# Norm weight in the evacuation, and sums spread between splits: two seams of a transformer layer kernel

## The chip, the cores and the metric

The kernel runs on one core of one Trainium2 chip. A core has a matrix engine (TensorE, PE below), a vector engine (VectorE, DVE), a scalar engine (ScalarE, ACT), GpSimd (POOL) and a queue engine (SyncE, SP), which work side by side, each in the order of its own instructions, and wait for each other by semaphores. SP and POOL issue the transfers (DMA) between HBM and the on-chip memory SBUF. PE writes its results into PSUM, from which ACT or DVE must fetch them ("evacuate") before the buffer is used again. The metric is the device time of one execution in microseconds (us).

## The reference

One layer of a streaming encoder runs on 1024 prompt tokens and 32 sample tokens, which share the weights. All numbers are fp32. Cut to what matters here:

```python
def rms_norm(x, g):
    xf = x.astype(jnp.float32)
    y = xf * lax.rsqrt(jnp.mean(xf * xf, axis=-1, keepdims=True) + EPS) * g.astype(jnp.float32)
    return y.astype(x.dtype)

def conv_ffn(h, conv_s0, w_up, conv_w, conv_b, w_down):
    a, g = jnp.split(h @ w_up, [D_FF], axis=-1)
    gx = jnp.concatenate([conv_s0.astype(g.dtype), g], axis=1)
    gc = conv_b + sum(conv_w[i] * gx[:, i:i + T] for i in range(CONV_W))
    y = (jax.nn.gelu(gc) * a) @ w_down
    return y, gx[:, T:]

def layer_forward(...):
    ...
    mix = (jax.nn.sigmoid(ga) * (oa @ w_br_a) + jax.nn.sigmoid(gb) * (ob @ w_br_b)) @ w_out
    x = x + rms_norm(mix, g_post_mix)
    f, conv_new = conv_ffn(rms_norm(x, g_pre_ffn), conv_s0, w_up, conv_w, conv_b, w_down)
    x = x + rms_norm(f, g_post_ffn)
    gate = jax.nn.sigmoid(rms_norm(x, g_pre_ple) @ w_ple_gate)
    x = x + rms_norm(gate * (pe @ w_ple), g_post_ple)
```

D_MODEL is 1024 and D_FF 2816. Ahead of this stand a gated linear attention and a banded softmax attention, which the change does not touch.

## The kernel before

Activations lie transposed: features on the 128 partitions, the 1056 tokens along the free axis. Where tokens are cut, there are three chunks of 352 (NC = 3, CW = 352) or two halves of 528, each taken as 2 x 264. PE multiplies fp32 as high and low parts: a value is split by ACT into a rounded high part (h, hi, mh, whi) and by DVE into the rest (l, lo, ml, wlo), and a product is three matmuls (high by high, high by low, low by high). A product of eight feature tiles is thus 24 matmuls.

**The out stage** (L1714 to L1739) computes z = mix @ w_out chunk by chunk, eight products a chunk (n = 0 to 7), with all of a chunk's z in one tile. Each product goes into one of four rotating PSUM buffers ("mm"). ACT copies it to z[:, n]; after each second product ACT squares the pair (L1607) and DVE adds the square to an accumulator. At the end of the chunk the generator norm_steps is made for it. It runs in 16 steps, called out of the next chunk's product loop by OUT_STEPS (so many steps after product n) and, for the last chunk, out of the plain up products by UP_STEPS. The steps are: the loads of the residual and the total of the accumulator (fold, L1621, and its split, L1632 and L1633); the inverse root (two matmuls with a matrix of ones that sum over partitions, L1638 and L1639, then log, exp and a Newton step, with a table load of ACT ahead, L239); four steps that multiply a pair of z's tiles by weight and root (times, L1656), add the residual (L1670) and square the result; the last square; its total; an empty step; the second inverse; four steps that multiply by the next norm's weight, spill z to d_hn, and split it into the rows of the up products (L1691 for the high part, L1685 for the low); and the last low part. Engines' orders are written out by hand here (manual_schedule for PE, DVE and ACT); SP's and POOL's come from a scheduler.

**The plain up products** follow (up_plain): the first three pairs of up tiles (f = 0 to 2; j = 0, 1 for the two halves of w_up), chunk by chunk, from the rows hh and hl. Out of their loop run the last chunk's norm and then plain_rest, which loads d_hn again (tiles hn, pool sp) and forms the quarter sums t1, t2 (and later t3, t4) for what comes next. The pool zp, with z, is released just before sp is made.

**The up stage** (up_strassen, f = 4 to FT - 1) multiplies quarters with seven products in place of eight. A product here is 24 matmuls of 264 columns into a PSUM pair (X, Y, Z, V, U). The activated rows go to HBM (d_b) for the down stage.

**The last up pair** (f = FT - 1) has a written order of its own: after X, Y, Z come V (rows t2), U (rows t1), and V again with t3 added. Eight DVE additions from PSUM finish it, three between the products (L1946, L1947, L1949) and five in a function ends() (L1953, L1954 and last_quarter, L1921 to L1923).

**The down stage** begins by loading rows (row_load, into sraw and uraw) and weights (w_load, raw and wraw) and splitting them (row_split: ACT L2050, DVE L2051, tiles d0 to d8; w_split: ACT L2099, DVE L2100). Rows (0, 0) and (0, 1) go into a buffer of the pool sw, the others into uraw, a tile of pool rp that exists only when the pools sp and mp have been released. Then 28 products u of 66 matmuls each run, 22 row tiles by 3 (L2356 to L2358).

Of the kernel before, what the change touches and what calls it, by code (L numbers as in the profile page):

```python
# [17 lines left out]
P = 128  # L18
# [84 lines left out]
RES_BUFS = 4  # L103
OUT_STEPS = (1, 1, 2, 2, 2, 1, 1, 5)
UP_STEPS = (1, 1, 2, 2, 2, 1, 1, 2, 3)

# [7 lines left out]
def emit(tc, a):  # L114
# [1511 lines left out]
    def norm_steps(tmp, c, z, acc, g, resid, keep, g_next, dst, spill=None):  # L1626
# [9 lines left out]
        def inverse(out, h, l):  # L1636
            ps = ps_one()[:, :CW]
            pe.matmul(ps, ones["D"], h, start=True, stop=False)  # L1638
            pe.matmul(ps, ones["D"], l, start=False, stop=True)  # L1639
            log_exp()  # L1640
            newton(out, ps, tmp)
# [11 lines left out]

        def times(i, g, r):
            for j in range(2):
                ve.scalar_tensor_tensor(zs[i][:, j], zs[i][:, j], col(g + 2 * i + j), r, op0=ALU.mult, op1=ALU.mult)  # L1656
# [63 lines left out]
    for c in range(NC):  # L1720
        s = chunk(c)
        z = tl(zp, [P, KT, CW], tag="z", bufs=2)
        acc = tl(zp, [P, 2, CW], tag="accz", bufs=1)
        for n in range(KT):
            hi, lo = wout[n]
            ps = ps_mm()
            product(ps[:, :CW], hi, lo, [(k, k) for k in range(KT)], lambda k: mh[:, k, s], lambda k: ml[:, k, s])
            if c == 0:
                out_weights(n + 2)
            else:  # L1730
                norm_part(OUT_STEPS[n])
            if c == NC - 1 and n in (4, 5):
                up_weights(0, n - 4)
            ac.activation(z[:, n], ps[:, :CW], AF.Copy)
            if n % 2:
                squares(zp, acc, n // 2, z[:, n - 1 : n + 1])
        norm = norm_steps(zp, c, z, acc, G_POST_MIX, a["x"], d_x1, G_PRE_FFN,
                          lambda i, s=s: [t[:, 2 * i : 2 * i + 2, s] for t in (hh, hl)], d_hn)
    wo.release()  # L1739

# [64 lines left out]
    def up_plain():  # L1805
        bufs = {}
        steps = [(f, j, c) for cs in ((0, 1), (2,)) for f in range(3) for j in range(2) for c in cs]

# [25 lines left out]
    def quarter_rows(k):  # L1834
        b = [tl(sp, [P, T], tag="hn", bufs=2) for i in range(2)]
        dma.dma_start(b[0], d_hn[k])
        dma.dma_start(b[1][:, two], d_hn[k + HK, :, two])
        return b[0][:, one], b[0][:, two], b[1][:, two]
# [6 lines left out]
    def quarter_sums():  # L1845
        for n in ("t1", "t2"):
            XS[n] = [tl(sp, [P, HK, HT], F32R, tag=n + x) for x in "hl"]
        for k in range(HK):
            b11, b12, b22 = quarter_rows(k)
            t1, t2 = [tl(sp, [P, HT], tag="xs", bufs=2) for i in range(2)]  # L1850
            ve.tensor_tensor(t1, b12, b11, op=ALU.subtract)
            ve.tensor_tensor(t2, b22, t1, op=ALU.subtract)
            dma.dma_start(d_t2[k], t2)
            quarter_split("t1", k, t1)
            quarter_split("t2", k, t2)
            yield

    def quarter_third():
        XS["t3"] = [tl(sw, [P, HK, HT], F32R, tag="t3" + x) for x in "hl"]
        for k in range(HK):  # L1860
            t = tl(sp, [P, T], tag="hn", bufs=2)
            dma.dma_start(t[:, one], d_hn[k, :, two])
# [6 lines left out]
    def quarter_last():  # L1869
# [4 lines left out]
        for k in range(HK):  # L1874
            t = tl(sp, [P, T], tag="hn", bufs=2)
            dma.dma_start(t[:, one], d_t2[k])
# [7 lines left out]
    def up_strassen(f):  # L1884
# [46 lines left out]
        if f == FT - 1:  # L1931
# [11 lines left out]
            V, U = ps_pair(), ps_pair()  # L1943
            V_, U_ = V[:, :, :HC], U[:, :, :HC]
            mul(V, weight(s2, WL_ENG[1]), "t2", True, True)
            ve.tensor_tensor(q, p1, V_, op=ALU.add)  # L1946
            ve.tensor_tensor(c12, c12, q, op=ALU.add)  # L1947
            mul(U, weight(s1, WL_ENG[2]), "t1", True, True)
            ve.tensor_tensor(c12, c12, U_, op=ALU.add)  # L1949
            mul(V, weight(s3, WL_ENG[4]), "t3", False, True)  # L1950

            def ends():
                ve.tensor_tensor(q, p1, V_, op=ALU.add)  # L1953
                ve.tensor_tensor(c21, c21, q, op=ALU.add)  # L1954
                last_quarter(q, U)

            return gx, av, ends
        Y = ps_pair()
# [18 lines left out]

    sp = None


    def plain_rest(bufs):
        nonlocal sp
        zp.release()
        sp = pool("sp", side="right")
        yield from quarter_sums()
        activate(0, *bufs[0, 0])
# [20 lines left out]
    order.__exit__(None, None, None)  # L2007
    quarter_last()
    for f in (2, 3):
        activate(f, *open_[f, 0])  # L2010
# [27 lines left out]
    def row_load(p, i):  # L2038
        if p < len(RSRC):
            n = 2 if i < 5 else 1  # L2040

            raws[p, i] = (sw_raw() if (p, i) < (0, 2) else tl(rp, [P, 2 * HT], tag="uraw", bufs=3)).rearrange("p (k t) -> p k t", k=2)[:, :n]
            dma.dma_start(raws[p, i], d_b[RSRC[p], 2 * i : 2 * i + n].rearrange("k p t -> p k t"))
# [251 lines left out]
    for i in range(1, 5):  # L2295
        row_load(0, i)
    for q in range(3):
        row_split(0, q)
        w_split(0, q)
    row_load(0, 5)  # L2300
    row_split(0, 3)
    row_load(1, 0)
    last_up[2]()
    row_split(0, 4)
    row_load(1, 1)
    sw.release()
    last_rows_up = activate_steps(FT - 1, *last_up[:2])
# [374 lines left out]
```

## Time and profile before

| | |
|---|---|
| runs | 1953.86, 1954.07, 1955.78 us, median 1954.07 |
| profiled execution | 1952.56 us, of which 1950.6 are the span of the trace |
| granted TensorE clock | 0.996 |
| PE busy | 1898.7 us, 97% of the span, 13960 matmuls |
| DVE busy | 1284.8 us, 66% |
| ACT busy | 931.5 us, 48% |
| POOL busy | 208.0 us, 11% |
| DMA | 300.91 MB, mean 154 GB/s |

In the span the out stage lies at about 1045 to 1140 us, the last up pair ends at about 1606 us, and the first down product follows at once. A row of an engine in order of time gives start, duration, engine, line, operation, output and inputs with shapes, and in brackets the idle time ahead of it with what ended it. Durations overlap on PE, since matmuls are pipelined; distances are read from starts. A row of PE's waits gives the line that waited, what it waited for, the total in us, how many times, and the longest.

### The profile page before, as it was taken

What the parts mean: (1) busy time and instruction counts of PE and PEld (TensorE: products, weight loads), DVE (VectorE), ACT (ScalarE), POOL (GpSimd) and SP (SyncE); (2) the same over time, 40 slices, a digit from 0 to 9 for tenths busy, and PEclk for the clock granted to TensorE, in tenths of its full rate; (3) what the DMA queues carried; (4) which work ended last, traced back from release to release, by engine and by line L of the source; (5) the groups of instructions that cost most, each with busy time, mean ns of one, the idle gap of its engine ahead of it and who ended that gap; (6) DMA issues with size and microseconds to landing.
All of it is one profiled execution on the core that took longest, in us unless ns stands there. A gap on an engine that the chain in (4) does not pass through costs nothing.

```text
span 1950.6 us, 34919 instructions
## 1 busy us (share of the span) xinstructions
PE 1898.7 (97%) x13960; PEld 1861.5 (95%) x13960; DVE 1284.8 (66%) x2367; ACT 931.5 (48%) x1820; POOL 208.0 (11%) x352
## 2 busy tenths in 40 slices
PE   8999999999999999999999999999999999999996
PEld 8999999989999999999999999999999999999996
DVE  6855444555656776777544686877777766558776
ACT  7444345556665455453333455433334345555555
POOL 0000000000001101001220121111111211000112
PEclk9999999999999999999999999999999999999998
DMA  7233335232315546567844246544354559897756
GB/s 279 85 100 111 99 104 156 82 89 81 91 47 154 145 120 160 161 182 216 303 133 127 90 162 205 185 138 138 113 125 111 125 146 304 266 297 240 239 158 106
DMA packets 111119, 300.91 MB, mean 154 GB/s; under 512 B 12452, under 2 KB 34796, under 8 KB 110316
## 3 DMA queue, kind: packets, MB, share of 16 engines
q1 hardware_dynamic: 81500, 205.95, 33.5%
q0 software_dynamic: 28016, 88.05, 16.7%
q10 hardware_dynamic: 1440, 4.69, 0.6%
q8 instruction: 109, 1.79, 0.4%
q14 instruction: 54, 0.44, 0.1%
HBM read 201.20 MB, written 114.09 MB: 162 GB/s over the span
## 4 chain that ended last, share of the span: by engine, by line
PE 76%; DVE 12%; ACT 7%; issue 2%; DMA 2%; ACTq 0%; SPq 0%; DVEq 0%
PE two L1911 6%; PE two L1913 6%; PE two L1912 6%; PE mm L230 5%; PE mm L232 5%; PE mm L231 5%; PE mm L804 4%; PE mm L805 4%; PE mm L806 4%; PE two L2358 4%; PE two L2357 4%; PE two L618 4%; PE two L619 3%; PE two L2356 3%; PE two L620 3%
## 5 line engine op out<-in xcount | busy, mean ns | idle before, releaser
L804 PE MATMUL mm<-xh,whi 128*128 128x352 f32 x696 | 236.6, 340 | 0.0
L806 PE MATMUL mm<-xh,wlo 128*128 128x352 f32 x696 | 225.3, 324 | 0.0
L805 PE MATMUL mm<-xl,whi 128*128 128x352 f32 x696 | 224.6, 323 | 0.0
L2357 PE MATMUL two<-d,whi 128*128 128x264 f32 x616 | 174.8, 284 | 2.7 <-DVE d L2051 2.7
L2358 PE MATMUL two<-d,wlo 128*128 128x264 f32 x616 | 175.5, 285 | 1.2 <-DVE wlo L2100 1.2
L2356 PE MATMUL two<-d,whi 128*128 128x264 f32 x616 | 174.7, 284 | 0.1
L1913 PE MATMUL two<-mh,wlo 128*128 128x264 f32 x576 | 163.0, 284 | 0.0
L1912 PE MATMUL two<-ml,whi 128*128 128x264 f32 x576 | 162.9, 284 | 0.0
L1911 PE MATMUL two<-mh,whi 128*128 128x264 f32 x576 | 161.2, 284 | 0.0
L804 PEld LDWEIGHTS mm<-xh,whi 128*128 128x128 f32 x696 | 131.3, 189 | 1.7
L805 PEld LDWEIGHTS mm<-xl,whi 128*128 128x128 f32 x696 | 131.2, 189 | 0.4
L806 PEld LDWEIGHTS mm<-xh,wlo 128*128 128x128 f32 x696 | 130.5, 188 | 0.0
L2357 PEld LDWEIGHTS two<-d,whi 128*128 128x128 f32 x616 | 115.8, 188 | 3.3 <-DVE d L2051 3.3
L2358 PEld LDWEIGHTS two<-d,wlo 128*128 128x128 f32 x616 | 115.6, 188 | 1.7 <-DVE wlo L2100 1.7
L2356 PEld LDWEIGHTS two<-d,whi 128*128 128x128 f32 x616 | 116.4, 189 | 0.3 <-ACT d L2050 0.3
L1913 PEld LDWEIGHTS two<-mh,wlo 128*128 128x128 f32 x576 | 108.4, 188 | 0.0
L1912 PEld LDWEIGHTS two<-ml,whi 128*128 128x128 f32 x576 | 108.4, 188 | 0.0
L1911 PEld LDWEIGHTS two<-mh,whi 128*128 128x128 f32 x576 | 107.3, 188 | 0.0
L940 ACT ACTIVATE s<-s,sm 128x640 f32<-128x640 f32 (+5 forms) x72 | 50.6, 703 | 97.1 <-DVE sm L939 97.0
L1901 ACT ACTIVATE whi<-ws 128x512 fp32r<-128x512 f32 x72 | 45.2, 631 | 97.9 <-PE two L1912 72.7
L618 PE MATMUL two<-th,whi 128*128 128x264 f32 x320 | 90.8, 284 | 0.0
L619 PE MATMUL two<-tl,whi 128*128 128x264 f32 x320 | 90.8, 284 | 0.0
(610 smaller groups left out, 5996.9 us busy)
## 6 DMA issues: line engine op xcount, KB each, us to landing
raw<-in_w_in SPq DMA_DIRECT2D x52, 512.0 KB, 3.7
uraw<-d_b SPq DMA_DIRECT2D x34, 528.0 KB, 4.6
d_b<-av POOLq DMA_DIRECT2D x33, 528.0 KB, 4.0
d_ws<-in_w_down POOLq DMA_DIRECT2D x24, 704.0 KB, 6.5
raw<-in_w_up SPq DMA_DIRECT2D x27, 512.0 KB, 3.6
wraw<-d_ws SPq DMA_DIRECT2D x16, 704.0 KB, 6.4
d_b<-gc POOLq DMA_DIRECT2D x11, 792.0 KB, 4.9
sraw<-in_w_up SPq DMA_DIRECT2D x17, 512.0 KB, 4.7
```

Source lines behind the costliest of these rows:

```text
L230: pe.matmul(ps, h, xh(kt), start=(first and i == 0), stop=False)
L618: pe.matmul(ps[:, j, :HC], w[0][:, k], x[0](k, s), start=st, stop=False, skip_group_check=True)
L619: pe.matmul(ps[:, j, :HC], w[0][:, k], x[1](k, s), start=False, stop=False, skip_group_check=True)
L804: pe.matmul(ps, wh, h[:, k, s], start=(k == 0), stop=False)
L805: pe.matmul(ps, wh, l[:, k, s], start=False, stop=False)
L806: pe.matmul(ps, wl, h[:, k, s], start=False, stop=(k == cnt - 1))
L1911: pe.matmul(ps[:, j, :HC], w[0][:, k], x[0][:, k, s], start=st, stop=False, skip_group_check=True)
L1912: pe.matmul(ps[:, j, :HC], w[0][:, k], x[1][:, k, s], start=False, stop=False, skip_group_check=True)
L1913: pe.matmul(ps[:, j, :HC], w[1][:, k], x[0][:, k, s], start=False, stop=sp_, skip_group_check=True)
L2356: pe.matmul(o, wh, xh_[:, s], start=(k == 0 and p in (0, 4, 5)), stop=False, skip_group_check=True)
L2357: pe.matmul(o, wh, xl_[:, s], start=False, stop=False, skip_group_check=True)
L2358: pe.matmul(o, wl, xh_[:, s], start=False, stop=(k == HD - 1 and p in (3, 4, 6)), skip_group_check=True)
```

## The change

**Out stage.** ACT now squares each product straight from PSUM into one half of a square tile, and then copies the product with the weight of the norm as a scale (one value per partition), so that z holds mix times g_post_mix while the squares are those of mix. times(i, None, r) therefore only multiplies by the root, one DVE instruction for a pair of tiles in place of two. The table load is taken out of inverse() and stands once behind the first chunk. The first step of norm_steps (loads and total) runs at the end of its own chunk, ahead of what remains of the norm before it. OUT_STEPS and UP_STEPS are changed to suit, and in up_plain the second half j = 1 of chunk 0 comes ahead of chunk 1 for the first pair.

**Down stage.** The tiles hn and xs move from the pool sp to a pool sh of their own, which is released before the up stage; the pool sx takes its place and holds the buffers of rows (0, 2) and (0, 3). The last up pair puts its t3 product into a PSUM pair W of its own, as V, W, U, and all additions move into ends(), now a generator of three steps that are called between the first splits of the down stage.

```diff
-OUT_STEPS = (1, 1, 2, 2, 2, 1, 1, 5)
-UP_STEPS = (1, 1, 2, 2, 2, 1, 1, 2, 3)
+OUT_STEPS = (1, 1, 1, 2, 2, 2, 2, 1)
+UP_STEPS = (0, 1, 2, 2, 2, 1, 2, 2, 2)
...
             pe.matmul(ps, ones["D"], l, start=False, stop=True)
-            log_exp()
             newton(out, ps, tmp)
...
         def times(i, g, r):
+            if g is None:
+                ve.tensor_tensor(zs[i], zs[i], r.unsqueeze(1).to_broadcast([P, 2, CW]), op=ALU.mult)
+                return
...
-            ac.activation(z[:, n], ps[:, :CW], AF.Copy)
-            if n % 2:
-                squares(zp, acc, n // 2, z[:, n - 1 : n + 1])
-        norm = norm_steps(zp, c, z, acc, G_POST_MIX, a["x"], d_x1, G_PRE_FFN,
+            if n % 2 == 0:
+                sq = acc if n == 0 else tl(zp, [P, 2, CW], tag="sq", bufs=2)
+            ac.activation(sq[:, n % 2], ps[:, :CW], AF.Square)
+            ac.activation(z[:, n], ps[:, :CW], AF.Copy, scale=col(G_POST_MIX + n))
+            if n == 3:
+                ve.scalar_tensor_tensor(acc, sq, 4 * EPS, acc, op0=ALU.add, op1=ALU.add)
+            elif n % 2 and n > 1:
+                ve.tensor_tensor(acc, acc, sq, op=ALU.add)
+        if c == 0:
+            log_exp()
+        rest = norm
+        norm = norm_steps(zp, c, z, acc, None, a["x"], d_x1, G_PRE_FFN,
                           lambda i, s=s: [t[:, 2 * i : 2 * i + 2, s] for t in (hh, hl)], d_hn)
+        next(norm)
+        for i in rest or ():
+            pass
...
-        steps = [(f, j, c) for cs in ((0, 1), (2,)) for f in range(3) for j in range(2) for c in cs]
+        steps = [(0, 0, 0), (0, 1, 0), (0, 0, 1), (0, 1, 1)]
+        steps += [(f, j, c) for cs in ((0, 1), (2,)) for f in range(3) for j in range(2) for c in cs if f or c == 2]
...
-            t = tl(sp, [P, T], tag="hn", bufs=2)
+            t = tl(sh, [P, T], tag="hn", bufs=2)
...
+            W = ps_pair()
+            W_ = W[:, :, :HC]
             mul(V, weight(s2, WL_ENG[1]), "t2", True, True)
-            ve.tensor_tensor(q, p1, V_, op=ALU.add)
-            ve.tensor_tensor(c12, c12, q, op=ALU.add)
+            mul(W, weight(s3, WL_ENG[4]), "t3", True, True)
             mul(U, weight(s1, WL_ENG[2]), "t1", True, True)
-            ve.tensor_tensor(c12, c12, U_, op=ALU.add)
-            mul(V, weight(s3, WL_ENG[4]), "t3", False, True)
             def ends():
                 ve.tensor_tensor(q, p1, V_, op=ALU.add)
+                ve.tensor_tensor(c12, c12, q, op=ALU.add)
+                yield
+                ve.tensor_tensor(q, q, W_, op=ALU.add)
                 ve.tensor_tensor(c21, c21, q, op=ALU.add)
+                yield
+                ve.tensor_tensor(c12, c12, U_, op=ALU.add)
                 last_quarter(q, U)
-            return gx, av, ends
+                yield
+            return gx, av, ends()
...
         sp = pool("sp", side="right")
+        for x in ("t1h", "t1l", "t2h", "t2l"):
+            tl(sp, [P, HK, HT], F32R, tag=x, bufs=1)
+        sh = pool("sh", side="right")
...
     quarter_last()
+    sh.release()
+    sx = pool("sx")
...
-            raws[p, i] = (sw_raw() if (p, i) < (0, 2) else tl(rp, [P, 2 * HT], tag="uraw", bufs=3)).rearrange("p (k t) -> p k t", k=2)[:, :n]
+            raws[p, i] = (sw_raw() if (p, i) < (0, 2) else tl(sx, [P, 2 * HT], tag=f"sraw{i}") if (p, i) < (0, 4) else tl(rp, [P, 2 * HT], tag="uraw", bufs=3)).rearrange("p (k t) -> p k t", k=2)[:, :n]
...
-    for q in range(3):
+    for q in range(2):
         row_split(0, q)
         w_split(0, q)
+    next(last_up[2])
+    row_split(0, 2)
+    w_split(0, 2)
+    next(last_up[2])
     row_load(0, 5)
     row_split(0, 3)
+    next(last_up[2])
     row_load(1, 0)
-    last_up[2]()
     row_split(0, 4)
     row_load(1, 1)
+    sx.release()
```

Where the orders differ. First PE at the seam of chunks 1 and 2 of the out stage, before. mm is a product's PSUM buffer (11927 is product 0 of chunk 2, 11966 product 1), one the sum over partitions, y the two parts of the total:

```order
L231 MATMUL mm_11966<-ml_10492,whi_11333 128x352
L232 MATMUL mm_11966<-mh_10491,wlo_11334 128x352
L1638 MATMUL one_11992<-y_1794_11961,onesDr_74 128x352
L1639 MATMUL one_11992<-y_1795_11962,onesDr_74 128x352
L230 MATMUL mm_12005<-mh_10491,ahi_11366 128x352
```

And after (11943 is product 0 of chunk 2, 11981 product 1):

```order
L231 MATMUL mm_11943<-ml_10492,whi_11323 128x352
L232 MATMUL mm_11943<-mh_10491,wlo_11324 128x352
L1638 MATMUL one_11969<-y_1791_11931,onesDr_74 128x352
L1639 MATMUL one_11969<-y_1792_11932,onesDr_74 128x352
L230 MATMUL mm_11981<-mh_10491,whi_11329 128x352
```

The two sums over partitions have moved from behind product 1 to behind product 0.

ACT at the same seam, before: z_11617 is chunk 1's z, z_11925 chunk 2's, mh_10491 <- z_11337 the high parts of chunk 0's normed rows, and L239 the table load:

```order
L1734 ACTIVATE z_11617<-mm_11839 128x352
L1691 ACTIVATE mh_10491<-z_11337 128x2x352 x4
L1734 ACTIVATE z_11617<-mm_11876 128x352
L1607 ACTIVATE sq_11922<-z_11617 128x704
L1632 ACTIVATE y_1794_11961<-accz_11618 128x352
L1734 ACTIVATE z_11925<-mm_11927 128x352
L239 ACT_TABLE_LOAD
L1595 ACTIVATE y_1799_11996<-one_11992 128x352
L1596 ACTIVATE y_1799_11996<-y_1799_11996 128x352
L1734 ACTIVATE z_11925<-mm_11966 128x352
```

And after, where L1738 and L1739 evacuate a product, and L1693 is what was L1691:

```order
L1738 ACTIVATE sq_11811<-mm_11814 128x352
L1739 ACTIVATE z_11635<-mm_11814,vec_69 128x352
L1693 ACTIVATE mh_10491<-z_11337 128x2x352 x2
L1738 ACTIVATE sq_11886<-mm_11852 128x352
L1739 ACTIVATE z_11635<-mm_11852,vec_69 128x352
L1693 ACTIVATE mh_10491<-z_11337 128x2x352
L1738 ACTIVATE sq_11886<-mm_11889 128x352
L1739 ACTIVATE z_11635<-mm_11889,vec_69 128x352
L1632 ACTIVATE y_1791_11931<-accz_11636 128x352
L1693 ACTIVATE mh_10491<-z_11337 128x2x352
L1595 ACTIVATE y_1798_11972<-one_11969 128x352
L1596 ACTIVATE y_1798_11972<-y_1798_11972 128x352
```

The high parts stand spread over three places instead of four in a row ahead of product 7, a product is squared before it is copied, the table load is gone, and the total's high part (L1632) stands ahead of the last high part.

DVE at the start of the down stage, before. two_17435 and two_17436 are the PSUM pairs V and U, c the tile q, av and gx the last up pair's outputs; d are row splits, wlo weight splits:

```order
L1946 TENSOR_TENSOR c_2428_17307<-p_2427_17306,two_17435 128x528
L1947 TENSOR_TENSOR av_17303<-av_17303,c_2428_17307 128x528
L1949 TENSOR_TENSOR av_17303<-av_17303,two_17436 128x528
L2051 TENSOR_TENSOR d_2460_17552<-sraw_17538,d_2460_17552 128x1056
L2100 TENSOR_TENSOR wlo_17556<-raw_17540,whi_17555 128x512
L2051 TENSOR_TENSOR d_2463_17559<-sraw_17544,d_2463_17559 128x1056
L2100 TENSOR_TENSOR wlo_17563<-raw_17540,whi_17562 128x512
L2051 TENSOR_TENSOR d_2466_17566<-uraw_17546,d_2466_17566 128x1056
L2100 TENSOR_TENSOR wlo_17570<-raw_17541,whi_17569 128x384
L2051 TENSOR_TENSOR d_2470_17575<-uraw_17548,d_2470_17575 128x1056
L1953 TENSOR_TENSOR c_2428_17307<-p_2427_17306,two_17435 128x528
L1954 TENSOR_TENSOR gx_17302<-gx_17302,c_2428_17307 128x528
```

And after, where L2075 is what was L2051 and L2124 what was L2100 (two_17441 is V, two_17443 W):

```order
L2075 TENSOR_TENSOR d_2465_17556<-sraw_17542,d_2465_17556 128x1056
L2124 TENSOR_TENSOR wlo_17560<-raw_17544,whi_17559 128x512
L2075 TENSOR_TENSOR d_2468_17563<-sraw_17548,d_2468_17563 128x1056
L2124 TENSOR_TENSOR wlo_17567<-raw_17544,whi_17566 128x512
L1966 TENSOR_TENSOR c_2432_17313<-p_2431_17312,two_17441 128x528
L1967 TENSOR_TENSOR av_17309<-av_17309,c_2432_17313 128x528
L2075 TENSOR_TENSOR d_2471_17572<-sraw_2462_17550,d_2471_17572 128x1056
L2124 TENSOR_TENSOR wlo_17576<-raw_17545,whi_17575 128x384
L1969 TENSOR_TENSOR c_2432_17313<-c_2432_17313,two_17443 128x528
L1970 TENSOR_TENSOR gx_17308<-gx_17308,c_2432_17313 128x528
L2075 TENSOR_TENSOR d_2475_17583<-sraw_2463_17552,d_2475_17583 128x1056
```

Two row splits and two weight splits have moved ahead of the additions, which now follow in pairs with a row split after each.

More of the change, by code (lines that the diff above doesn't have):

```diff
@@ L1834, in quarter_rows @@
     def quarter_rows(k):
-        b = [tl(sp, [P, T], tag="hn", bufs=2) for i in range(2)]
+        b = [tl(sh, [P, T], tag="hn", bufs=2) for i in range(2)]
         dma.dma_start(b[0], d_hn[k])
@@ L1846, in quarter_sums @@
         for n in ("t1", "t2"):
-            XS[n] = [tl(sp, [P, HK, HT], F32R, tag=n + x) for x in "hl"]
+            XS[n] = [tl(sp, [P, HK, HT], F32R, tag=n + x, bufs=1) for x in "hl"]
         for k in range(HK):
             b11, b12, b22 = quarter_rows(k)
-            t1, t2 = [tl(sp, [P, HT], tag="xs", bufs=2) for i in range(2)]
+            t1, t2 = [tl(sh, [P, HT], tag="xs", bufs=2) for i in range(2)]
             ve.tensor_tensor(t1, b12, b11, op=ALU.subtract)
@@ L1874, in quarter_last @@
         for k in range(HK):
[L1875 removed]
+            t = tl(sh, [P, T], tag="hn", bufs=2)
             dma.dma_start(t[:, one], d_t2[k])
@@ L1976, in up_strassen @@
         activate(f, gx, av)
-    sp = None
+    sp = sh = None
     def plain_rest(bufs):
-        nonlocal sp
+        nonlocal sp, sh
         zp.release()
         sp = pool("sp", side="right")
+        for x in ("t1h", "t1l", "t2h", "t2l"):
+            tl(sp, [P, HK, HT], F32R, tag=x, bufs=1)
+        sh = pool("sh", side="right")
         yield from quarter_sums()
```

## The prediction

> **What bounds the kernel now.** I read the page's totals first, then what TensorE (PE) waited for, then the rows of PE, ACT and DVE in order of time around each wait of the two stages that the change touches.
>
> ```profile
> span 1950.6 us, 34919 instructions
> PE 1898.7 (97%) x13960; PEld 1861.5 (95%) x13960; DVE 1284.8 (66%) x2367; ACT 931.5 (48%) x1820; POOL 208.0 (11%) x352
> ```
>
> PE carries the time. The change neither adds nor drops a matmul, so all it can win is idle time of PE, and all it can lose is new idle time there. PE's waits, by line (total, times, longest):
>
> ```profile
> PE two L2357 <- DVE d L2051: 2.7, 3, 1.6
> ...
> PE one L1638 <- ACT y L1632: 2.0, 2, 1.2
> ...
> PE mm L231 <- DVE ml L1685: 1.7, 3, 0.6
> PE two L2358 <- DVE wlo L2100: 1.2, 2, 1.0
> ```
>
> L1638 and the waits on ml lie in the out stage and the up products right behind it, L2357 and one wait of L2358 at the start of the down stage. Nothing else in reach waits. A wait also costs a restart, so I add up the starts of PE's rows. The out stage:
>
> ```profile
> 1114.08 0.32 PE L232 MATMUL mm<-mh,wlo 128*128 128x352 f32 x1
> 1115.23 0.43 PE L1638 MATMUL one<-y,onesDr 128*128 128x352 f32 x1 [0.83 <-ACT y L1632]
> 1115.79 0.43 PE L1639 MATMUL one<-y,onesDr 128*128 128x352 f32 x1
> 1116.05 0.32 PE L230 MATMUL mm<-mh,ahi 128*128 128x352 f32 x1
> 1116.21 0.32 PE L231 MATMUL mm<-ml,ahi 128*128 128x352 f32 x1
> ...
> 1149.52 0.32 PE L232 MATMUL mm<-mh,wlo 128*128 128x352 f32 x1
> 1151.02 0.43 PE L1638 MATMUL one<-y,onesDr 128*128 128x352 f32 x1 [1.17 <-ACT y L1632]
> ```
>
> Unhindered, 352-column matmuls start 0.16 us apart (the last two rows of the first group). The gaps of 1.15, 0.56 and 0.26 us lose 1.5 us. At 1149.5 the gap of 1.50 loses 1.34, with the same 0.5 for the two followers 1.85. The three waits on ml are 1.7 us by the waits view; with some 0.3 of restart each I take 2.6. Together **6.0 us**. The down stage:
>
> ```profile
> 1611.42 0.39 PE L2357 MATMUL two<-d,whi 128*128 128x264 f32 x1 [0.69 <-DVE d L2051]
> ...
> 1614.76 0.39 PE L2357 MATMUL two<-d,whi 128*128 128x264 f32 x1 [1.62 <-DVE d L2051]
> ...
> 1617.21 0.39 PE L2357 MATMUL two<-d,whi 128*128 128x264 f32 x1 [0.35 <-DVE d L2051]
> ...
> 1627.32 0.39 PE L2358 MATMUL two<-d,wlo 128*128 128x264 f32 x1 [0.97 <-DVE wlo L2100]
> 1627.55 0.28 PE L2356 MATMUL two<-d,whi 128*128 128x264 f32 x1
> 1627.67 0.28 PE L2357 MATMUL two<-d,whi 128*128 128x264 f32 x1
> ```
>
> Starts are 0.12 us apart here, and a restart makes the next one 0.23 (last three rows). The first three waits are 2.66 us and, with 0.4 for restarts and their followers each, 3.9; the fourth is 1.25. Together **5.1 us**. So 11.1 us (0.57%) is the most that the change can win here.
>
> **The out stage.** What ACT and DVE did at the end of chunk 1, before L1638 of 1115.23 could start:
>
> ```profile
> 1107.60 0.80 ACT L1691 ACTIVATE mh<-z 128x704 fp32r<-128x704 f32 x1 [0.20 <-DVE z L1656]
> ...
> 1111.19 0.79 ACT L1691 ACTIVATE mh<-z 128x704 fp32r<-128x704 f32 x1 [1.00 <-DVE z L1656]
> 1111.89 0.45 ACT L1734 ACTIVATE z<-mm 128x352 f32<-128x352 f32 x1
> 1112.37 0.79 ACT L1607 ACTIVATE sq<-z 128x704 f32<-128x704 f32 x1
> 1114.68 0.50 ACT L1632 ACTIVATE y<-accz 128x352 fp32r<-128x352 f32 x1 [1.52 <-DVE accz L1621]
> ...
> 1115.55 1.28 ACT L239 ACT_TABLE_LOAD   x1
> 1116.84 0.46 ACT L1595 ACTIVATE y<-one 128x352 f32<-128x352 f32 x1
> ```
>
> ```profile
> 1105.49 2.07 DVE L1656 SCALAR_TENSOR_TENSOR z<-z,vec,rstd 128x352 f32<-128x352 f32 x4
> ...
> 1113.19 0.89 DVE L1614 TENSOR_TENSOR accz<-accz,sq 128x704 f32<-128x704 f32 x1 [0.29 <-ACT sq L1607]
> 1114.12 0.53 DVE L1621 TENSOR_TENSOR accz<-accz 128x352 f32<-128x352 f32 x1
> 1115.21 0.53 DVE L1633 TENSOR_TENSOR y<-accz,y 128x352 fp32r<-128x352 f32 x1 [0.56 <-ACT y L1632]
> ```
>
> L1638 stands two products (48 matmuls, 7.8 us) behind the chunk's last one, which therefore ended at about 1114.24 - 7.8 = 1106.5. Its evacuation began only at 1111.89, 5.4 us late: ACT was busy with the mh splits of the norm before, which waited for DVE. From there evacuation, square, add, fold and splits of the total take until 1115.74, 3.85 us.
>
> In the new order the square reads PSUM, so the add follows 0.45 after the evacuation begins, not 1.30, and the chain takes about 3.0 us. Three of the four mh splits stay ahead of the evacuation, but spread over products 6 and 7; the fourth goes behind the total. L1638 moves one product up, so the cover is one product, 3.9 us. Carrying all engines forward with these durations (a start is when engine and inputs are free) I estimate y's low part ready against wanted by PE: chunk 0, 1078.3 against 1078.8; chunk 1, 1110.2 against 1110.5; chunk 2, 1143.9 against 1146.1, as there two up products stand ahead. The second inverse, now behind product 5 and not 6, comes at 1098.1 against 1098.5. Everything is in time, three places by 0.3 to 0.5 us only. The waits on ml also go: the up products ask for chunk 1's rows third, not second, and I find the last ml at 1146.6 against 1149.4. Gain 5.8, with 0.2 left for a missed margin.
>
> What the new forms cost: the evacuation with a scale from a vector lies between the plain one, 0.45 in the row at 1111.89, and this one, which is the same operation on another tile:
>
> ```profile
> L1051 ACT ACTIVATE ev<-one,vec 128x352 f32<-128x352 f32 x9 | 5.0, 556 | 0.0
> ```
>
> I take 556 ns: 24 times 0.10 is 2.4 us of ACT, and 24 squares of 0.45 replace 12 of 0.79, 1.3 us more. Against it stand five loads of 1.28 us fewer, 6.4. ACT is idle for 1.0 to 1.5 us between the rows above, so none of it is on PE's path. On DVE a broadcast multiply, 0.89 by the 704-wide add, replaces two multiplies of together 1.04 (half of the 2.07): a small gain at cover.
>
> [...]
>
> The new pools let the first hn load (quarter sums) wait for all spills of the last norm.
>
> ```profile
> 1182.56 0.33 SPq L1836 DMA_DIRECT2D hn<-d_hn  x1
> ...
> 1204.67 0.46 SPq L1863 DMA_DIRECT2D hn<-d_hn  x1
> ...
> 1219.05 0.33 SPq L1862 DMA_DIRECT2D hn<-d_hn  x1
> ```
>
> It goes out about 4 us later against PE. Behind it on DVE and ACT stand the quarter sums and the t1 and t2 splits, and behind those, in order, the evacuations of the up products, which by my estimate then lag PE by up to 4.9 us. The products rotate through four PSUM buffers, so PE notices only when it is three products, 11.6 us, ahead. The 14 us in which SP issues no hn load after 1204.67 take up the delay before the quarters are wanted. The cost lies between 0 and the whole 4 us; I take 0, since the lag stays below half of what PE allows.
>
> **The down stage.** DVE, then ACT, around its start:
>
> ```profile
> 1603.35 0.70 DVE L1949 TENSOR_TENSOR av<-av,two 128x528 f32<-128x528 f32 x1 [1.44 <-PE two L1913]
> 1603.97 1.25 DVE L2051 TENSOR_TENSOR d<-sraw,d 128x1056 fp32r<-128x1056 f32 x1
> ...
> 1610.11 1.26 DVE L2051 TENSOR_TENSOR d<-uraw,d 128x1056 fp32r<-128x1056 f32 x1 [0.86 <-ACT d L2050]
> ```
>
> ```profile
> 1598.02 1.08 ACT L2050 ACTIVATE d<-sraw 128x1056 fp32r<-128x1056 f32 x1
> ...
> 1608.98 1.09 ACT L2050 ACTIVATE d<-uraw 128x1056 fp32r<-128x1056 f32 x1 [5.07 <-DMA uraw<-d_b]
> ```
>
> DVE could not split the first rows (d, 1603.97) before three adds of the last up pair, and the fourth came at 1610.11 because its rows landed late (5.07 us of ACT waiting for the transfer). The change loads rows 2 and 3 long before and puts the adds between the splits. d's first split on ACT gets a new wait, on V's last matmul (its buffer overlaps t2's low part): 1600.3 instead of 1598.0. DVE then has d0 at 1601.4, d1 about 1603, the first two adds at 1605, d2 at 1606.4, two adds at 1608, d3 at 1609.5 to 1610.7, the last adds, d4 at 1612.0 to 1613.3. PE still begins at 1606.0, waits 0.37 at d3 and 1.09 at d4: 1.46 left of 3.86. The first product ends 2.4 us sooner, d5 is in time, and the wait of 1627.32 goes too, as wlo there comes at 1623.1 against 1623.5. Gain 3.65.
>
> The eight adds are the same; the second product's weights land at about 1611.4, before they are wanted. What can be late next is the fifth weight block, which ACT met at 1640.48 by a wait on its transfer; I leave 0.3 us for it.
>
> **Sum.** -5.8 - 3.65 + 0.3 = -9.15 us: span 1941.5, profiled execution 1943.4 against 1952.56. The median of the runs lies 1.5 above the profiled execution, so the median comes to **1945.0 us**.
>
> **Rivals.** A: the margins fail. Each of the three thin places that misses pays a wait of up to 0.8 and a restart of 0.5; with all three 3.9 us are given back, 1949. For it: margins below one ACT instruction. Against: L1638 runs six times in the stage and waited only twice even behind the late evacuations of the old order.
>
> B: the down stage does not gain, as the transfers set it.
>
> ```profile
> 1597.00:1605.00 8.00, 8.00 (x68) 8.00 (x68) 3.06 (x4) 5.10 (x7) 2.06 (x2) 1.00 0.97 236
> ```
>
> The DMA share in this window is 0.97 (last but one number), and if the weight blocks then come no sooner, 3.65 is lost again: 1948.6. Against: 1.06 MB of rows (two loads) leave this stretch for an earlier one, at the 236 GB/s of the window 4.5 us of transfer, more than the 3.65 by which PE runs ahead. [...]
>
> C: neither holds, since ml and the adds only wait elsewhere: A and B together, with 2 us of new waits, 1954.
>
> D, slower: the late hn load blocks ACT. ACT and DVE work in order, so a t1 split that waits for hn holds up the evacuations behind it. It decides once the lag passes 11.6 us, and 9.15 + 3.9 = 13 us of PE idle must come from it, so a lag of 24.7 us, to end 0.2% slower; 1958 or more. Only if every hn load, not the first, waited on spills, would that be reached.
>
> **Chances.** Forecast 0.66 (its own range 1943 to 1947), A 0.11, B 0.09, C 0.07, D 0.07. By 0.2% (3.9 us, about what can be told from no change), faster is below 1950.2: forecast, A and B without the upper edge of the last two, 0.82. Same: C and that edge, 0.10. Slower: D and C's upper edge, 0.08. The range: 1942 is the forecast without the 1.46 us of down waits and with both small allowances (0.5) and some margin of addition (1 us) on the good side; 1951.5 takes in A, B and two thirds of what both together give back.
>
> **What would show it.** After: no wait of L1638 over 0.3 us; none on ml behind the out stage; one table load in the out stage; the scaled evacuation at about 556 ns; the first d split on ACT beginning with V's end; two waits of L2357 on d of 0.4 and 1.1 us, none on wlo at the third product. Wrong would make it a wait on y or on PSUM in the up products, ACT idle on hn for over 10 us, or a new wait for wraw in the down stage.

## The result, and the profile after

The changed kernel takes 1951.42 us (median of 22 runs, 1947.11 to 1953.22) against 1954.08 us of the kernel before (22 runs). The ratio is 0.9982, 95% interval 0.9975 to 0.9988: 3.5 us less, where 9.1 were forecast; the medians alone are 2.7 us apart. Of the runs below, one execution of the version with z swapped took 4720.55 us and is left out of its ratio. The profiled execution of the changed kernel takes 1948.54 us with a span of 1946.7 us, 3.9 less than the span before.

PE's waits in the changed kernel, those of the stages in question:

```profile
PE two L1925 <- DVE gx L1937: 1.5, 1, 1.5
...
PE one L232 <- DVE wlo L210: 1.0, 1, 1.0
PE two L1927 <- DVE wlo L1916: 0.9, 1, 0.9
PE two L2386 <- DVE d L2075: 0.8, 1, 0.8
...
PE two L2387 <- DVE wlo L2124: 0.3, 1, 0.3
```

The waits that the change aimed at are gone or small: none on L1638, none on ml, in the down stage 0.8 us on d where there were 2.7, and none on wlo at its third product where there was 1.0. (The 0.3 on wlo lies at 1829.1, near the end of the stage, and stood in the kernel before as well: 0.27 at 1832.9, part of its 1.2.) But three waits are new. They lie between the two stages, in the first up tiles: L232 at 1211 us, L1927 at 1314.8 and L1925 at 1316.8.

Where the time went can be read from the first and last start of three groups of matmuls. The kernel before (columns behind the count: shortest, median, longest duration in ns, then first and last start in us):

```profile
L230 PE MATMUL mm<-mh,whi x128: 318/325/425, 1043.9 to 1237.3; 128*128 128x352 f32 x128
L1912 PE MATMUL two<-t2l,whi x144: 278/283/293, 1240.8 to 1600.0; 128*128 128x264 f32 x144
L2356 PE MATMUL two<-d,whi x616: 279/284/389, 1606.1 to 1837.6; 128*128 128x264 f32 x154
```

And the changed kernel:

```profile
L230 PE MATMUL mm<-mh,whi x128: 318/325/330, 1045.3 to 1234.1; 128*128 128x352 f32 x128
L1926 PE MATMUL two<-t2l,whi x144: 280/285/293, 1237.6 to 1599.9; 128*128 128x264 f32 x144
L2385 PE MATMUL two<-d,whi x616: 279/284/337, 1606.0 to 1833.8; 128*128 128x264 f32 x154
```

The first group starts with the out stage, t2l runs through the up stage, d through the down stage. I call the distance from the first start of mh to the first of t2l "out" (it holds the plain up products too), from the first to the last t2l "up", and from the first to the last d "down":

| | out | up | down |
|---|---|---|---|
| before | 196.9 | 359.2 | 231.5 |
| changed | 192.3 | 362.3 | 227.8 |

So 4.6 us were won in the first part, 3.1 lost in the second and 3.7 won in the third. The out stage itself begins 1.4 us later than before; that comes from far ahead of the change, and the last section tells from what.

The parts that the change was made of behave as written. ACT's groups, with the mean in ns:

```profile
L239 ACT ACT_TABLE_LOAD x11 | 14.1, 1283 | 0.2
L1739 ACT ACTIVATE z<-mm,vec 128x352 f32<-128x352 f32 x24 | 13.2, 550 | 1.4 <-DVE rs L1599 1.4
```

Five table loads fewer, and the scaled evacuation takes 550 ns. At the start of the down stage, ACT and then DVE:

```profile
1600.22 1.09 ACT L2074 ACTIVATE d<-sraw 128x1056 fp32r<-128x1056 f32 x1 [2.21 <-PE two L1926]
```

```profile
1601.34 1.26 DVE L2075 TENSOR_TENSOR d<-sraw,d 128x1056 fp32r<-128x1056 f32 x1 [4.96 <-ACT d L2074]
...
1609.31 1.25 DVE L2075 TENSOR_TENSOR d<-sraw,d 128x1056 fp32r<-128x1056 f32 x1
...
1611.84 1.25 DVE L2075 TENSOR_TENSOR d<-uraw,d 128x1056 fp32r<-128x1056 f32 x1
```

The first split waits for V's last matmul (2.21 us, until 1600.22), and d0, d3 and d4 come at 1601.3, 1609.3 and 1611.8.

What lies behind the new waits is the activation of the up tiles. Its first instruction on ACT (gc<-gx, L1763 before) waits for the spill of the gc before it, since there is one buffer. Before:

```profile
1295.37 1.27 ACT L1763 ACTIVATE gc<-gx,vec 128x1058 f32<-128x1058 f32 x1 [3.76 <-DMA d_b<-gc]
...
1311.00 1.28 ACT L1763 ACTIVATE gc<-gx,vec 128x1058 f32<-128x1058 f32 x1 [2.30 <-DMA d_b<-gc]
```

And changed:

```profile
1293.85 1.28 ACT L1776 ACTIVATE gc<-gx,vec 128x1058 f32<-128x1058 f32 x1 [5.41 <-DMA d_b<-gc]
...
1311.55 1.28 ACT L1776 ACTIVATE gc<-gx,vec 128x1058 f32<-128x1058 f32 x1 [6.04 <-DMA d_b<-gc]
```

PE is 3.2 us earlier here than before (1237.6 against 1240.8), the activation at 1311 is 0.55 us later: 3.75 us lost between them. Behind it in ACT's and DVE's order stand the weight split and the last quarter (L1935 to L1937) for which PE waits at 1314.8 and 1316.8. The spill that ended this wait, from the transfers issued between 1299 and 1313 us (KB, median us to landing), before:

```profile
d_b<-gc POOLq DMA_DIRECT2D x1, 792.0 KB, 4.9
```

And changed:

```profile
d_b<-gc POOLq DMA_DIRECT2D x1, 792.0 KB, 7.0
...
sraw<-d_b SPq DMA_DIRECT2D x1, 528.0 KB, 7.1
```

The row load sraw<-d_b is one of the two that the change issues early. It started 0.9 us behind the spill (1305.37 and 1304.45). How much of the spill's longer time it makes, the experiments tell.

### The profile page after: what moved, and what is told of

Its sections match the earlier page's. It is cut to its first block, busy times and chain, and to the rows that moved or that the text cites. A ratio compares the mean times of both kernels' runs of the same rounds, so it can differ in the third digit from the quotient of the medians.

```text
span 1946.7 us, 34924 instructions
## 1 busy us (share of the span) xinstructions
PE 1897.9 (97%) x13960; PEld 1862.1 (96%) x13960; DVE 1281.4 (66%) x2355; ACT 926.1 (48%) x1827; POOL 209.0 (11%) x352
## 4 chain that ended last, share of the span: by engine, by line
PE 78%; DVE 12%; ACT 7%; issue 2%; DMA 1%; SPq 0%; ACTq 0%; DVEq 0%
PE mm L230 6%; PE mm L232 6%; PE mm L231 6%; PE two L1925 6%; PE two L1926 6%; PE two L1927 6%; PE mm L804 4%; PE mm L805 4%; PE mm L806 4%; PE two L618 4%; PE two L619 4%; PE two L620 3%; PE two L2387 3%; PE two L2386 3%; PE two L2385 3%
## 5 line engine op out<-in xcount | busy, mean ns | idle before, releaser
L1927 PE MATMUL two<-mh,wlo 128*128 128x264 f32 x576 | 163.3, 285 | 0.9 <-DVE wlo L1916 0.9
L1925 PE MATMUL two<-mh,whi 128*128 128x264 f32 x576 | 161.4, 285 | 1.5 <-DVE gx L1937 1.5
L1927 PEld LDWEIGHTS two<-mh,wlo 128*128 128x128 f32 x576 | 108.5, 188 | 1.1 <-DVE wlo L1916 1.1
L1925 PEld LDWEIGHTS two<-mh,whi 128*128 128x128 f32 x576 | 107.3, 188 | 1.7 <-DVE gx L1937 1.7
L620 PE MATMUL two<-th,wlo 128*128 128x264 f32 x320 | 90.6, 284 | 0.0
```

What stands on the lines that cost most here:

```text
L620: pe.matmul(ps[:, j, :HC], w[1][:, k], x[0](k, s), start=False, stop=sp_, skip_group_check=True)
L1925: pe.matmul(ps[:, j, :HC], w[0][:, k], x[0][:, k, s], start=st, stop=False, skip_group_check=True)
L1927: pe.matmul(ps[:, j, :HC], w[1][:, k], x[0][:, k, s], start=False, stop=sp_, skip_group_check=True)
```

## The experiments

The theory on which they were made: two things push the activations behind PE, the first hn load that now waits for the last norm's spills, and the row load beside a spill. Its rival: the activations are bound by their spills anyway, so that PE cannot keep what it wins in the out stage. All times below are against the kernel before on the same chip.

**Row loads back in their old place.**

```diff
-            raws[p, i] = (sw_raw() if (p, i) < (0, 2) else tl(sx, [P, 2 * HT], tag=f"sraw{i}") if (p, i) < (0, 4) else tl(rp, [P, 2 * HT], tag="uraw", bufs=3))...
+            raws[p, i] = (sw_raw() if (p, i) < (0, 2) else tl(rp, [P, 2 * HT], tag="uraw", bufs=3))...
```

> The changed kernel, but rows (0,2) and (0,3) are loaded as before, once the pools of the up stage are free. Theory 1 (two small costs of the new pools push the chain of activations behind PE: the row load that shares the transfers with the spill of gc, and the first hn load that waits for the last norm's spills): the spill of gc at about 1304 us lands in about 4.9 us again, not 7.0, and PE's waits at 1314 to 1317 shrink from 2.7 to at most 1.0; the wait of 1.0 on wlo at 1211 stays. In the down stage the rows come late again, waits on d of 2 to 3 us return: total within 1.5 us of the changed kernel. Theory 2 (the out stage's gain cannot be kept, since the activations of the first up tiles are bound by their spills whatever the pools): the waits at 1314 to 1317 stay above 2 us.

Ratio 0.9997 (0.9988 to 1.0007): all of the gain is lost. Its waits:

```profile
PE two L2386 <- DVE d L2075: 1.7, 3, 0.8
...
PE two L1925 <- DVE gx L1937: 1.5, 1, 1.5
PE two L2387 <- DVE wlo L2124: 1.2, 2, 1.0
PE two L2385 <- ACT d L2074: 1.1, 1, 1.1
```

Out, up and down are 192.2, 361.4 and 231.6. The down stage is where it was before, so without the early rows the new order of the additions wins nothing. Of the two waits in the up tiles the one on wlo is gone, the one of 1.5 us on gx stays; the spill took 6.2 us, not the 4.9 expected. My bound of 1.0 for what would remain was wrong: the row load is a cause, not the only one.

**Chunk 2's z in the other buffer.** A dummy tile turns the two z buffers, so that hn lies where chunk 1's z was.

```diff
+    po.memset(tl(zp, [P, KT, CW], tag="z", bufs=2)[:, 0, :2], 0.0)
     for c in range(NC):
         s = chunk(c)
         z = tl(zp, [P, KT, CW], tag="z", bufs=2)
```

> The changed kernel with a dummy tile ahead of the out stage, so that chunk 2's z lies in the other buffer and the hn buffers lie where chunk 1's z was; the first hn load then waits only for the data that it reads. Theory 1: the first hn load goes out 3 to 4 us sooner, the wait on wlo at 1211 is gone (1.1 us), the first activation starts 3 us sooner, and the waits at 1314 to 1317 fall below 1.0: 3 us less than the changed kernel, ratio to before about 0.9965. Theory 2: the wait on wlo goes, the waits at 1314 to 1317 stay above 2 us: ratio about 0.9977.

Ratio 0.9955 (0.9937 to 0.9972). The first hn load on SP in the changed kernel, and behind it the same in this one:

```profile
1181.84 0.33 SPq L1850 DMA_DIRECT2D hn<-d_hn  x1
```

```profile
1175.55 0.33 SPq L1851 DMA_DIRECT2D hn<-d_hn  x1
```

It goes out 6 us sooner against PE (61.8 us ahead of the first t2l product, where the changed kernel has 55.8). The wait on wlo at 1211 is gone, and out is 191.0, 1.3 us less. In the up tiles one wait is left:

```profile
PE two L1926 <- DVE gx L1938: 1.5, 1, 1.5
```

So here too one of the two causes, the row load, is enough for a wait of 1.5 us. The fall below 1.0 that I expected did not come. The up part of this profile is 363.0, 3.8 more than before: besides the wait it has a stretch of 3.4 us at a granted clock of 0.50, which the last section shows.

**The out stage's part alone**, with pools, row loads and last up pair as before (the first five pieces of the diff, the last of them the order in up_plain).

> Only the out stage's part of the change (evacuation, table load, steps, order of the up products), with pools, row loads and last up pair of before. Theory 1: all of the 6 us of the out stage is kept, no wait on wlo at 1211, at most 0.5 us of waits at 1314 to 1317; down stage as before; ratio about 0.9970. Theory 2: waits of 2 us or more in the first up tiles; ratio about 0.9982.

Ratio 0.9961 (0.9947 to 0.9976). Out is 191.0, up 359.1, down 231.3: all of the 5.9 us of the out stage are kept, and no wait lies in the up tiles. The waits of the down stage are those of before:

```profile
PE two L2371 <- DVE d L2065: 2.1, 3, 1.6
...
PE two L2372 <- DVE wlo L2114: 1.3, 2, 1.0
```

The rival falls with it: PE runs 5.9 us ahead and the activations keep pace. Measured from the first t2l product, the activation that stands at 1311 in the rows above begins 70.4 us behind it here and 70.2 before, but 73.9 in the changed kernel, and 73.1 and 73.0 in the two runs that leave one cause.

**The other part alone**, with the out stage and up_plain as before.

> Only the other part (pools, rows ahead, last up pair's order), with the out stage of before. Theory 1: the late hn load and the row load cost 2 to 4 us of waits in the first up tiles though PE is no earlier than before; the down stage gains 3.7; ratio 0.9985 to 1.0005. Theory 2: no waits in the first up tiles, since PE is not ahead; ratio about 0.9981.

Ratio 0.9989 (0.9980 to 0.9998); 198.7, 360.7 and 227.8. The new waits come although PE is no earlier than before:

```profile
PE one L232 <- DVE wlo L210: 1.3, 1, 1.3
...
PE two L1911 <- DVE gx L1923: 1.0, 1, 1.0
```

They are a cost of the new pools and of the rows loaded early into them. The part wins 3.7 us in the down stage and gives 3.3 back ahead of it.

**The row loads held back.** With z swapped, two small copies write into the rows' buffers behind the activation of f = 9, and the loads wait for them.

```diff
     sx = pool("sx")
+    SX = {i: tl(sx, [P, 2 * HT], tag=f"sraw{i}") for i in (2, 3)}
...
         last_up = up_strassen(f)
+        if f == UP_PLAIN + 5:
+            for t in SX.values():
+                po.tensor_copy(t[:, :4], convo[:, f])
```

> The changed kernel with chunk 2's z in the other buffer (as in the run that swaps z) and the loads of rows (0,2) and (0,3) held back by two small POOL copies until the activation of f = 9 has passed. Theory 1 in its second form (each of the two small costs alone is enough for a wait of 1.5 us at about 1315, none is left without both): no wait on wlo at 1211, none on gx at about 1315, waits in the down stage as in the changed kernel (0.8 and 0.3); ratio to before about 0.9950. Rival (the loads do harm wherever they stand in the up stage): a wait of 1 us or more at some later f, ratio about 0.9965.

Ratio 0.9955 (0.9943 to 0.9968); 191.0, 359.4, 227.7, and no wait in the up tiles. The spill that took 7.1 us with a row load beside it (z swapped) takes 4.6 here. With neither cause left nothing is lost there, and later in the up stage (1352 us) the same loads harm nothing.

**A second gc buffer**, all else as in the changed kernel.

```diff
-        gc = tl(fp, [P, GW - 2], tag="gc", bufs=1)
+        gc = tl(sx if 4 <= f < FT - 1 and f % 2 == 0 else fp, [P, GW - 2], tag="gc", bufs=1)
```

> The changed kernel with a second buffer for gc (even f from 4 on take theirs from the pool of the rows), hn and row loads left as in the changed kernel. If the waits at 1314 to 1317 come from the activation that waits for the spill of the gc before it, they are gone though both causes stay; the wait on wlo at 1211 (1.0) stays: ratio about 0.9965. If they come from the transfers or the DVE order itself, they stay above 1.5 us: ratio 0.998.

Ratio 0.9955 (0.9941 to 0.9968); 192.0, 359.4, 227.8. ACT's activations no longer wait for a spill:

```profile
1260.24 1.26 ACT L1776 ACTIVATE gc<-gx,vec 128x1058 f32<-128x1058 f32 x1
...
1297.40 1.28 ACT L1776 ACTIVATE gc<-gx,vec 128x1058 f32<-128x1058 f32 x1 [0.28 <-DVE gx L1994]
```

The waits in the up tiles are gone, though hn comes as late as in the changed kernel (first load at 1182.1). As the late hn alone was enough for a wait of 1.5 us, this shows that the wait on the spill was the way by which it reached PE. For the row load the run shows less: it still goes out early, but at 1293.3 and no longer beside the later spill (1308.0), which took 5.0 us. The wait on wlo at 1211 stays (0.67 us), as it comes from hn alone.

**Both, the best version.** z swapped and a second gc buffer, rows early.

> Both: chunk 2's z in the other buffer, and a second buffer for gc; rows (0,2) and (0,3) loaded as in the changed kernel. By theory 1 no wait in the first up tiles at all and the down stage's gain kept: ratio about 0.9950, one group of times and not two. By the rival (transfers) a wait of about 1.5 us at 1315: ratio about 0.996.

Ratio 0.9950 (0.9938 to 0.9963), median 1944.78 of five runs between 1943.41 and 1944.93; 191.0, 359.3, 227.8. The changed kernel had 0.9955 to 0.9981 on this chip (next run), which overlaps, so the parts and the waits tell the two apart better than the times. The stretch that had the waits, PE at work all through (the last three numbers are granted clock, DMA share and GB/s):

```profile
1300.00:1320.00 20.00, 20.00 (x167) 20.00 (x166) 14.37 (x24) 7.21 (x12) 2.78 (x6) 1.00 0.33 114
```

**The changed kernel once more**, for a second profile.

> The changed kernel itself, for a second profile. Its times fell into two groups, about 1948.5 and 1952.5. If a granted clock of one half behind the waits at 1314 to 1317 makes the difference, a profile of a run near 1952.5 shows it there (3.3 us at half clock), one near 1948.5 does not. If the two groups come from elsewhere, both show the same clock there.

Ratio 0.9968 (0.9955 to 0.9981) here, five runs between 1944.83 and 1953.34 us. The profiled execution took 1953.34 us, with 192.1, 365.6 and 227.7: up is 3.3 us longer than in the first profile. The granted clock in the stretch of the waits (third last number):

```profile
1316.00:1318.00 2.00, 0.51 (x2) 0.30 (x2) 2.00 (x4) 0.12 (x1) 0.00 (x0) 0.91 0.00 0
1318.00:1320.00 2.00, 1.36 (x6) 1.36 (x7) 1.59 (x5) 2.00 (x3) 0.52 (x4) 0.50 0.02 4
1320.00:1322.00 2.00, 2.00 (x11) 2.00 (x11) 2.00 (x5) 0.01 (x1) 0.72 (x1) 0.50 0.01 2
1322.00:1324.00 2.00, 2.00 (x11) 2.00 (x11) 1.93 (x4) 0.00 (x0) 0.77 (x1) 0.50 0.92 351
1324.00:1326.00 2.00, 2.00 (x17) 2.00 (x16) 1.60 (x3) 0.63 (x1) 0.00 (x0) 0.89 0.91 323
```

From 1317.6, still inside the last of the waits, the granted clock was 0.50 for some 7 us. In the first profile, of an execution of 1948.54 us, the clock stayed at 1.00 there. The times of the changed kernel form two groups, 1947.1 to 1949.8 and 1951.3 to 1953.2 us in the 22 runs, with medians 4.3 us apart; the best version's lie within 1.5 us. The two profiled executions differ by 4.8 us, 3.3 in the up part and 1.3 ahead of the out stage. That the half clock makes most of the difference between the groups is likely, but only one execution of the upper group was seen in a profile, and of the five runs here one (1944.83) lies below both groups.

Three more runs start from the best version and undo one piece each. Their times differ from its times by less than the intervals, so what a piece is worth is read from one profile each. Parts that a run does not touch agree between profiles to 0.1 us: out is 191.0 in five of them, down 227.7 or 227.8 in nine.

**The last up pair as before**, rows early (V, U, V again, the additions ahead of and behind the splits, as in the code before).

> The version with z swapped and two gc buffers, but with the last up pair and the places of its additions as before; rows (0,2) and (0,3) still come early. Tells what the order of the additions is worth once the rows are there. If the early rows alone make the down stage's gain: PE's waits on d stay near 0.8 us in all. If the additions in front of the splits matter too: DVE reaches the first d about 2.6 us later (1604.0 against 1601.3 in the changed kernel), and PE waits 1 to 3 us more there, at the second to fourth row.

Ratio 0.9955 (0.9940 to 0.9970), down 228.3 against 227.8. One wait on d is left in the down stage, twice as long as in the changed kernel:

```profile
1610.39 0.39 PE L2378 MATMUL two<-d,whi 128*128 128x264 f32 x1 [1.61 <-DVE d L2071]
```

The wait is 0.8 us longer, just under the 1 to 3 that I expected if the order matters. The early rows make 3.2 of the 3.7 us; the order of the additions adds the rest, and only with them.

**A table load in every inverse again.**

```diff
+            log_exp()
             newton(out, ps, tmp)
...
-        if c == 0:
-            log_exp()
```

> The same version with a table load in every inverse root again (five more of 1.28 us on ACT). By the prediction's margins (0.3 to 0.5 us at three places) the loads would make L1638 or ml late: waits of 0.8 to 2.6 us in the out stage. If the margins are wider than estimated, or the loads lie beside other work: no wait, same time.

Ratio 0.9965 (0.9952 to 0.9978), out 192.8, 1.8 more. L1638 or L1639 come late at three places, by starts 0.6, 0.4 and 0.8 us with their followers. The last, with the row ahead of it, where starts 0.16 us apart would be unhindered:

```profile
1167.81 0.32 PE L232 MATMUL mm<-mh,alo 128*128 128x352 f32 x1
1168.27 0.42 PE L1638 MATMUL one<-y,onesDr 128*128 128x352 f32 x1
1168.83 0.43 PE L1639 MATMUL one<-y,onesDr 128*128 128x352 f32 x1
```

**The old evacuation**, new steps and one table load kept (the evacuation's lines and G_POST_MIX in norm_steps as before).

> The same version with the old evacuation (plain copy, square of a pair from SBUF, two multiplies with weight and root), the new steps and the single table load kept. The chain to the total is 0.85 us longer; by the margins of 0.3 to 0.5 us L1638 waits 0.4 us or more at two or three places, 1 to 2.5 us with restarts. If the steps alone make the gain: no wait over 0.3 us.

Ratio 0.9954 (0.9938 to 0.9971), out 191.4, 0.4 more than the best version. L1639 starts late at two places, by 0.07 us behind chunk 0 and by 0.34 behind chunk 1, where I expected waits of 0.4 or more at two or three. The second:

```profile
1111.01 0.37 PE L1638 MATMUL one<-y,onesDr 128*128 128x352 f32 x1
1111.51 0.43 PE L1639 MATMUL one<-y,onesDr 128*128 128x352 f32 x1
```

So of the 5.9 us of the out stage the table loads hold 1.8 and the new evacuation 0.4, when each is taken away alone; the larger rest is left for the steps and the order of the up products, which were not tried by themselves.

## Why the prediction was wrong

The direction was right, the size was not: 9.1 us forecast, 3.5 (interval 2.3 to 4.9) measured. The median, 1951.42, lies just below the upper end of the range that I gave, but that end was set for rivals that did not come, so this is luck. (The sum itself gives a median of 1944.9, which I wrote as 1945.0.)

*The out stage, "Gain 5.8".* Right: 5.9 wherever the pools did not spoil it. The estimated margins held: L1638 waits nowhere in the changed kernel. The run with the table loads shows that they were real and thin, since 1.28 us more in the inverses cost 1.8 us. The run with the old evacuation shows them somewhat wider than I had them: with a chain longer by 0.85 us, as I estimated it, one place came 0.34 us late and one 0.07.

*The down stage, "Gain 3.65".* Right: 3.7. Of the waits left, 1.46 by the forecast, 0.78 came at d4 and none at d3. The allowance of 0.3 us for late weight blocks was not needed.

*The first hn load, "I take 0".* This is the first step that failed. I saw the wait, and the delay of 4 us came out: the load goes out 0.7 us sooner than before (1181.84 against 1182.56) while PE is 4.5 us ahead (1166.9 against 1171.3 at the last L1638). Without the wait (z swapped) it goes out 6 us sooner still. But I asked only what the evacuations of the up products would make of it, by PSUM buffers. In DVE's order, behind the quarter sums, stands also the activation of f = 0, and behind that the weight split for which PE waits at 1211:

```profile
1210.09 0.71 DVE L1798 TENSOR_TENSOR gc<-av 128x528 f32<-128x528 f32 x1
1210.71 2.49 DVE L210 TENSOR_TENSOR wlo<-raw,whi 128x512 fp32r<-128x512 f32 x4
```

That is 1.0 us of wait and 1.3 of the out part. The activation of f = 0 begins 34.1 us ahead of the first t2l product, with z swapped 36.2, and the next ones are 1 to 2.4 us later as well. "The 14 us in which SP issues no hn load after 1204.67 take up the delay before the quarters are wanted" holds for the quarters, for which PE waits nowhere, but says nothing on the activations, which were already waiting for spills before the change (3.76 and 2.30 us in the rows above).

*The early row loads.* This is the second: "The change loads rows 2 and 3 long before" has no price and no cover named. I counted the 1.06 MB as leaving the down stage and not as arriving anywhere. The first arrived beside the spill of gc on which ACT was waiting. With z swapped the spill took 7.1 us with this load and 4.6 without it; in the changed kernel it took 7.0 with it and 6.2 without, against 4.9 before. Why it took 6.2 with the late hn alone stays open. In the two runs with z swapped, the load that SP issued lengthened the spill that POOL had issued: 7.1 us against 4.6.

Either cause alone gives a wait of 1.5 us at 1315 (the runs with rows in the old place and with z swapped), both together two waits of 0.9 and 1.5 us, and none is left without both or with a second gc buffer. In the first profile the up part is 3.1 us longer than before: 2.4 of waits, and restarts for most of the rest.

*What the sum over profiles missed.* In the second profile the granted clock fell to 0.50 at the last of the waits in the up tiles, for 6.8 us, and the up part was 3.3 us longer than in the first. This may be why the medians differ by less (2.7 us) than the best executions do (4.3); no term of mine had it.

Of the rivals, A and C did not come and B is refuted by the 227.8 us. D had the right place, the late hn load that holds up ACT and DVE, but I let it decide only by PSUM buffers and only for an end slower than before. A wait of a few us with that cause, which eats half of the gain, was none of the cases.

## What to carry to other kernels

A load that is moved away from a crowded stretch lands in another one: look up which transfer an engine is already waiting for there, since it can lengthen that wait (here a spill from 4.6 to 7.1 us). When an instruction gets a new wait, follow every kind of work behind it in the engine's order to the first point where the bound engine meets it; here the evacuations had room and the activations, bound by a single buffer and its spill, had none. A stage whose bound engine shows no wait can still be without slack, and the idle time of another engine before the same transfer, in the profile before, says so.

## What the runs showed of the hardware

Around some short waits of PE, of 1.5 to 2.0 us, the granted clock fell to 0.50. In the run with z swapped, a wait of 1.47 us ended at about 1315.6, and then the granted clock (third last number) fell:

```profile
1317.00:1318.00 1.00, 1.00 (x7) 1.00 (x6) 1.00 (x4) 0.00 (x0) 0.32 (x1) 0.50 0.00 0
...
1320.00:1321.00 1.00, 1.00 (x9) 1.00 (x9) 0.97 (x2) 0.63 (x1) 0.00 (x0) 0.90 0.82 304
```

It was at 0.50 from 1316.8 to 1320.2, 3.4 us. Matmuls of 264 columns start 0.22 us apart in that stretch and 0.12 ahead of it, so by my estimate some 1.5 us is lost there on top of the wait. In the second profile of the changed kernel it was at 0.50 for 6.8 us. Waits of about 1.5 us came with this in some executions and not in others (with the rows in their old place the clock stayed at 1.00 behind a wait of 1.5 us). What decides is not shown here.

The same lies far ahead of the change, behind a wait of 2.0 us of PE that both kernels have and that ends near 599.5 us. The kernel before, and then the changed one:

```profile
600.00:602.00 2.00, 2.00 (x17) 2.00 (x15) 1.34 (x4) 1.98 (x9) 0.55 (x1) 1.00 0.34 42
```

```profile
600.00:602.00 2.00, 2.00 (x8) 2.00 (x8) 1.30 (x4) 1.81 (x9) 0.47 (x1) 0.50 0.42 59
```

Eight matmuls in 2 us where there were seventeen, those of 352 columns 0.29 us apart by their starts and not 0.16: this makes 1.3 of the 1.4 us by which the out stage begins later in the changed kernel's profile. Nothing was changed there, so a comparison of two single profiles can be off by that much.
